# A two-layer transformer trunk on one core: inverse sums in the outputs' bank, norms by head, a two-queue launch and 512-column memory products

## The chip, the cores and the metric

The kernel runs on one core of a Trainium2 chip. The core has TensorE (PE, matrix products; its weight loads are listed as PEld), VectorE (DVE), ScalarE (ACT), GpSimd (POOL) and SyncE (SP, which issues DMAs here). Products accumulate in PSUM, eight banks of 512 fp32 columns for each of 128 partitions. The metric is the device time of one execution in microseconds, the median of several runs; lower is better.

## The reference

All is float32: 512 tokens of 1024 features, a memory of 256 tokens, two layers.

```python
for layer in range(DEPTH):                      # 2
    x = x + 0.5 * _swiglu(_rmsnorm(x, ffn_pre_norm[layer]), ffn_pre_w_gu[layer], ffn_pre_w_down[layer])
    h = _rmsnorm(x, mix_norm[layer])
    if layer % 2 == 0:
        x = x + _even_mixer(h, ...)             # stick-breaking attention and a gated unit
    else:
        x = x + _mla_mixer(h, positions, ...)   # 16 heads, low-rank q and kv
    x = x + _memory_cross_attention(_rmsnorm(x, xmem_norm[layer]), _rmsnorm(mem, xmem_mem_norm[layer]), ...)
    x = x + 0.5 * _swiglu(_rmsnorm(x, ffn_post_norm[layer]), ...)
```

The two places inside that matter here:

```python
# _mla_mixer: q and k are normed head by head (96 wide), then causal softmax attention
q = _rmsnorm(q, q_g)
k = _rmsnorm(k, k_g)
p = jax.nn.softmax(jnp.where(causal, sc, -jnp.inf), axis=-1)
# _memory_cross_attention: 4 heads of 256
k, v = jnp.split((hm @ wkv).reshape(b, m, MEM_HEADS, 2 * MEM_HEAD_DIM), 2, axis=-1)
k = _rmsnorm(k, k_g)
```

## The kernel before

x lies transposed in SBUF: eight tiles x0 to x7 of 128 features by 512 tokens. Every product is done with both operands split into a rounded high part and a low rest: `mm3` (L101) issues three products, high x high (L103), high x low (L104) and low x high (L105). `prep` (L122) makes hh and hl of x times the norm's gain; the norm's factor per token is applied later. `squares` (L136) sums x squared over the tiles into sqs; `stats` (L147) turns sqs into the factor per token (a product of 1 column by ones, then `rsqrt`, L107, a chain of some eleven small DVE operations), and `spread` (L164) copies it over all partitions into rbc.

Weights come in granules of at most 512 KB. `gran` (L85) loads one (three raw buffers), ACT casts the high part wh, and POOL (in two halves) or DVE subtracts for the low part wl (four buffers each).

The kernel's text is not the order of execution: a scheduler orders each engine's instructions by the order of the text and by when it expects their inputs. `with self.queued()` ties the PE instructions of a block behind the last mm3 issued so far. At run time each engine runs its list in order.

The stages, with their time in the profile: ffn, the even mixer, memory attention of layer 0 (its products from 592.90 us), two ffn, the MLA mixer, memory attention of layer 1 (from 1752 us), ffn.

- Launch: `constants` (L60) issues on SP the gains gc, the first weight granule (its low part made by DVE) and x0 to x7. `run` (L1112) does eight preps and eight squares. In `ffn` (L211) each product pair (gate pg, up pu) takes two PSUM banks of a pool of five; two more banks belong to psA, used by the down products, and one to the statistics. In the first ffn `stats` follows product 1 and `spread` product 2 (s0, L218).
- MLA attention (`mla_attn`, L654). Fill work, `filler`, projects q and kv for four groups of four heads (eight steps a group), then `first_half` begins the output product. `proj_q` and `proj_kv` square their result on ACT into a tile dg (one buffer), and DVE reduces it (L693, L719). When a group is complete, `norms` makes the factors, `knorm` (L670) scales all four heads of k at once, on DVE for group 0 and on POOL for the others, and POOL scales q (L700). The loop over n (L908) does, for head n: `scores` of n; for head n - 1 `weights`, which transposes the exponentials (L845) into banks of the tag pt (two banks) and copies them to wT; then `ahead`, which turns q and k of head n + 2 by transposes (L740), also into pt. In an even round two heads are complete: `inverse` transposes the inverse sums ar into a pt bank (L864), `spread` multiplies them out into the same bank (L872) and ACT copies it to rbc; `values` multiplies with v into the one bank of the tag av (L887), scales by rbc into a buffer of the tag sq, and splits. `take` puts fill steps between: FILL[n] has three counts, after the first weights, before `spread`, and at the round's end.
- Memory products (`memkv`, L959). Eight products in the order K0, K1, V0, K2, V1, K3, V2, V3; each has 256 columns, two token blocks in one bank, and two granules of four k-tiles. After the first: the memory's own statistics (L996) and `stats` of x (L1001). K products get tk (ACT), its squares, `rsqrt`, a scaling on DVE; `fin` transposes tk (L1026) two products later. V products get tv and a split. PSUM: three banks mm, three at, two psA.

Of the kernel before, what the change touches and what calls it, by code (L numbers as in the profile page):

```python
# [26 lines left out]
class Trunk:  # L27
# [32 lines left out]
    def constants(self):  # L60
        nc, cp, a = self.nc, self.cp, self.a
        self.gc = self.t(cp, [P, 10, KT], "gc")
        nc.sync.dma_start(out=self.gc, in_=a["gcols"])

        self.first = self.gran(a["w_gu0"][0], KT, P, lo="dve") if self.stop in (None, 1) else None
        self.x = [self.t(self.xp, [P, S], f"x{f}") for f in range(KT)]
        for f in range(KT):
# [3 lines left out]
        self.ones = self.t(cp, [P, P], "ones")  # L71
        nc.vector.memset(self.ones, 1.0)
        self.rbc = self.t(cp, [P, S], "rbc")

    def split(self, hi, lo, src, eng_hi="act", eng_lo="dve"):
# [7 lines left out]
        e.tensor_tensor(out=lo, in0=src, in1=hi.bitcast(F32), op=ALU.subtract)  # L83

# [126 lines left out]
    def ffn(self, w_gu, w_dn, g_next, out=None):  # L211
        nc, tc = self.nc, self.tc
        with tc.tile_pool(name=self.nm("ffn"), bufs=1) as fp, \
# [4 lines left out]
            s0 = 1 if self.first else 0  # L218
# [14 lines left out]
            for half in range(2):  # L233
                acts = []
                for j in range(H):
                    jj = half * H + j
                    pg = self.t(pp, [P, S], "mm")
                    pu = self.t(pp, [P, S], "mm")
                    for ps, w in ((pg, w_gu[jj]), (pu, w_gu[NFF + jj])):
                        wh, wl = self.first or self.gran(w, KT, P)  # L240
# [413 lines left out]
    def mla_attn(self, p, pl, pp, cT, krr, skr, gqk, neg, tq, o):  # L654
# [15 lines left out]
        def knorm(st, y, eng):  # L670
            st["ks"] = ks = self.t(p, [P, NT, G, 96], "ks", bufs=2)
            by = lambda d: y[:, :, :, None].to_broadcast([P, NT, G, d])
            eng.tensor_tensor(out=ks[:, :, :, 0:64], in0=st["kn"], in1=by(64), op=ALU.mult)
            eng.tensor_tensor(out=ks[:, :, :, 64:96], in0=krr[:, :, None, :].to_broadcast([P, NT, G, 32]), in1=by(32),
                              op=ALU.mult)

        def proj_kv(st, g, t):
# [22 lines left out]
            nc.gpsimd.tensor_tensor(out=st["qs"], in0=st["qs"], in1=st["s"][:, :, :, None].to_broadcast([P, NT, G, 96]),  # L700
                                    op=ALU.mult)

        def proj_q(st, g, t):
# [13 lines left out]
            s1 = self.t(self.sp, [P, NT, P], "dg", bufs=1)[:, :, 0:96]  # L717
# [137 lines left out]
        def inverse(sm):  # L855
# [7 lines left out]
            ps = self.t(pp, [P, S], "pt", bufs=2)  # L863
# [15 lines left out]
        def values(n, wTs, rb):  # L879
# [13 lines left out]
            w = self.t(self.sp, [P, S], "sq", bufs=2)  # L893
# [14 lines left out]
        for n in range(17):  # L908
# [50 lines left out]
    def memkv(self, p, pp, l, kT, V, gqk):  # L959
# [22 lines left out]
        for n, c in enumerate((0, 2, 1, 4, 3, 6, 5, 7)):  # L982
            h = c // 2
            ps = self.t(pp, [P, MT, 256], "mm")
            for hf in range(2):
                wh, wl = self.gran(a["xmem_wkv"][l, c * 2 + hf], 4, 256, lo="dve")
                for k in range(4):
                    kk = hf * 4 + k
                    for m in range(MT):
                        cs = slice(m * P, (m + 1) * P)  # L990
                        self.mm3(ps[:, m, :], (mh[kk][:, cs], ml[kk][:, cs]), (wh[:, k, :], wl[:, k, :]),
                                 kk == 0 and m == 0, kk == KT - 1)
            if rm is None:
                st = self.t(pp, [P, S], "at")
# [6 lines left out]
                self.stats(pp, "at")  # L1001
            while fins and fins[0][0] <= n - 2:
                with self.queued():
                    fins.pop(0)[1]()
            if c % 2 == 1:
                tv = self.t(p, [P, MT, 256], "tv", bufs=2)
                for m in range(MT):
                    nc.scalar.activation(out=tv[:, m, :], in_=ps[:, m, :], func=AF.Copy, scale=rm[:, m:m + 1])
                self.split(*V[h], tv, "dve", "pool")
                continue  # L1010
            tk = self.t(p, [P, MT, 256], "tk", bufs=2)
            ss = self.t(p, [P, MT], "kss", bufs=2)
            scr = self.t(p, [P, 256], "kscr", bufs=2)
            for m in range(MT):
                nc.scalar.activation(out=tk[:, m, :], in_=ps[:, m, :], func=AF.Copy, scale=rm[:, m:m + 1])
                nc.scalar.activation(out=scr, in_=tk[:, m, :], func=AF.Square, accum_out=ss[:, m:m + 1])
            rk = self.rsqrt(ss, MT, 1.0 / 256, EPS)
            for m in range(MT):
                nc.vector.tensor_scalar(out=tk[:, m, :], in0=tk[:, m, :], scalar1=rk[:, m:m + 1], scalar2=None,
                                        op0=ALU.mult)  # L1020

            def fin(tk=tk, h=h):
                for d in range(2):
                    pt = self.t(pp, [P, S], "at")
                    for m in range(MT):
                        nc.tensor.transpose(out=pt[:, m * P:(m + 1) * P], in_=tk[:, m, d * P:(d + 1) * P],  # L1026
                                            identity=self.ident)
                    hi, lo = kT[h][d]
# [177 lines left out]
```

## Time and profile before

| What | us |
|---|---|
| median of 3 runs | 2297.13 |
| the runs | 2290.03, 2297.13, 2308.14 |
| profiled execution | 2289.97 |
| its span | 2288.3 |
| mean granted TensorE clock in it | 0.997 |
| ACT busy in MLA attention, 1552 to 1735 (183) | 104.77 |
| DVE busy in MLA attention | 110.42 |
| DVE busy in the memory products of layer 0 (48.10) | 36.03 |
| ACT busy there | 28.49 |

A row of a list of waits reads: engine, tile and line that waited, what released it, us in total, times, longest. A row of a timeline reads: start, duration, engine, line, operation, output <- inputs, shapes, count, and in brackets the idle time before with its releaser. A PE duration holds the pipeline's depth; how far apart two products start says what one costs. A granted clock of 1.00 is full speed of TensorE. A row with several counts (x4) covers instructions one after another.

### The profile page before, as it was taken

Reading aid. Unit: us, or ns where it says so; the run is one execution under the profiler, and the core shown is the slowest. Engines: PE = TensorE matmul, PEld = TensorE weight load, DVE = VectorE, ACT = ScalarE, POOL = GpSimd, SP = SyncE. Lnnn points to the kernel's source line nnn. Section 1 sums busy time; section 2 is a strip of 40 time slices with the busy share of each in tenths; the row PEclk is TensorE's granted clock in tenths of the full one; section 3 lists DMA queues with packets and bytes.
Section 4 is the critical chain, followed back from the end, with each engine's and each line's share of the span. In section 5 each row is a group of like instructions: output and inputs, shape, how many; then the busy total and the mean of one; then the engine's idle time right before and its main releaser. Section 6 shows DMA issues by size and latency. Waiting matters only on the chain. (4 is left out here: it accounts for less than half of the span.)

```text
span 2288.3 us, 29129 instructions
## 1 busy us (share of the span) xinstructions
PE 2250.2 (98%) x11240; PEld 1885.1 (82%) x11240; DVE 907.2 (40%) x1686; ACT 867.4 (38%) x1443; POOL 1018.3 (45%) x824
## 2 busy tenths in 40 slices
PE   8999999999999999999999999998889999999999
PEld 6888888977988888888888888897668988888887
DVE  5211323466745422123422022376558555221220
ACT  4222333366544332223322232356546544322221
POOL 5545546212243454554554554635322424545543
PEclk9999999999999999999999999999999999999999
DMA  4323324211421332332332332321003412323222
GB/s 157 96 83 111 98 80 128 88 56 57 144 97 63 92 99 82 114 94 82 111 95 83 110 100 79 105 83 51 28 29 111 134 61 83 101 77 117 93 82 93
DMA packets 67354, 208.68 MB, mean 91 GB/s; under 512 B 8592, under 2 KB 10640, under 8 KB 67216
## 3 DMA queue, kind: packets, MB, share of 16 engines
q1 hardware_dynamic: 67216, 206.83, 29.3%
q8 instruction: 88, 1.44, 0.3%
q14 instruction: 50, 0.41, 0.1%
HBM read 204.70 MB, written 2.10 MB: 90 GB/s over the span
## 5 line engine op out<-in xcount | busy, mean ns | idle before, releaser
L97 POOL TENSOR_TENSOR wl<-wr,wh 128x512 fp32r<-128x512 f32 (+2 forms) x752 | 945.9, 1279 | 1083.2 <-ACT wh L92 1083.1
L92 ACT CAST wh<-wr 128x1024 fp32r<-128x1024 f32 (+3 forms) x423 | 408.0, 965 | 1040.2 <-PE mm L104 578.8
L103 PE MATMUL mm<-hh,wh 128*128 128x512 f32 x1424 | 556.6, 391 | 6.8 <-ACT hh L130 6.8
L104 PE MATMUL mm<-hl,wh 128*128 128x512 f32 x1424 | 555.6, 390 | 0.5 <-DVE hl L131 0.5
L105 PE MATMUL mm<-hh,wl 128*128 128x512 f32 x1424 | 555.5, 390 | 0.0
L103 PEld LDWEIGHTS mm<-hh,wh 128*128 128x128 f32 x1424 | 268.2, 188 | 62.3 <-ACT hh L130 6.8
L104 PEld LDWEIGHTS mm<-hl,wh 128*128 128x128 f32 x1424 | 268.2, 188 | 56.8 <-DVE hl L131 1.0
L105 PEld LDWEIGHTS mm<-hh,wl 128*128 128x128 f32 x1424 | 268.2, 188 | 56.2 <-POOL wl L97 0.3
L103 PE MATMUL A<-ah,wh 128*128 128x512 f32 x704 | 277.4, 394 | 0.0
L105 PE MATMUL A<-ah,wl 128*128 128x512 f32 x704 | 276.0, 392 | 0.0
L104 PE MATMUL A<-al,wh 128*128 128x512 f32 x704 | 273.2, 388 | 0.0
L226 DVE TENSOR_TENSOR t<-mm,rbc 128x512 f32<-128x512 f32 x88 | 60.9, 692 | 394.9 <-PE mm L105 394.9
L259 DVE SCALAR_TENSOR_TENSOR x<-A,x 128x512 f32<-128x512 f32 x64 | 44.3, 692 | 358.0 <-PE A L105 358.0
L105 PEld LDWEIGHTS A<-ah,wl 128*128 128x128 f32 x704 | 132.1, 188 | 31.0
L104 PEld LDWEIGHTS A<-al,wh 128*128 128x128 f32 x704 | 132.2, 188 | 29.6
L103 PEld LDWEIGHTS A<-ah,wh 128*128 128x128 f32 x704 | 132.3, 188 | 26.3
L224 DVE TENSOR_TENSOR t<-mm,rbc 128x512 f32<-128x512 f32 x88 | 60.9, 692 | 195.4 <-PE mm L105 188.5
L83 DVE TENSOR_TENSOR al<-t,ah 128x512 fp32r<-128x512 f32 x88 | 82.9, 942 | 60.4 <-ACT ah L79 60.4
L103 PE MATMUL A<-hh,wh 128*128 128x512 f32 x240 | 96.7, 403 | 0.0
L105 PE MATMUL A<-hh,wl 128*128 128x512 f32 x240 | 94.0, 392 | 0.0
L104 PE MATMUL A<-hl,wh 128*128 128x512 f32 x240 | 93.8, 391 | 0.0
L103 PE MATMUL mm<-wh,hh 128*128 128x256 f32 (+1 forms) x288 | 82.2, 285 | 0.0
(331 smaller groups left out, 3224.2 us busy)
## 6 DMA issues: line engine op xcount, KB each, us to landing
wr<-in_w_gu SPq DMA_DIRECT2D x176, 512.0 KB, 3.6
wr<-in_w_dn SPq DMA_DIRECT2D x64, 384.0 KB, 3.1
wr<-in_w_dn SPq DMA_DIRECT2D x64, 320.0 KB, 2.9
wr<-in_xmem_wkv SPq DMA_DIRECT2D x32, 512.0 KB, 3.3
wr<-in_xmem_wq SPq DMA_DIRECT2D x16, 512.0 KB, 3.3
wr<-in_xmem_wo SPq DMA_DIRECT2D x16, 512.0 KB, 3.2
wr<-in_sbg_w_zv SPq DMA_DIRECT2D x12, 512.0 KB, 3.6
wr<-in_sbg_w_qk SPq DMA_DIRECT2D x8, 512.0 KB, 3.6
```

The lines of the kernel that those rows point to most:

```text
L83: e.tensor_tensor(out=lo, in0=src, in1=hi.bitcast(F32), op=ALU.subtract)
L92: nc.scalar.copy(out=hi, in_=raw)
L97: e.tensor_tensor(out=lo_[:, c], in0=raw[:, c], in1=hi[:, c].bitcast(F32), op=ALU.subtract)
L103: mm(out, lhsT=A[0], rhs=B[0], start=start, stop=False, skip_group_check=True)
L104: mm(out, lhsT=A[0], rhs=B[1], start=False, stop=False, skip_group_check=True)
L105: self.pe = mm(out, lhsT=A[1], rhs=B[0], start=False, stop=stop, skip_group_check=True)
L224: nc.vector.tensor_tensor(out=t1, in0=pg, in1=self.rbc, op=ALU.mult)
L226: nc.vector.tensor_tensor(out=t2, in0=pu, in1=self.rbc, op=ALU.mult)
L259: nc.vector.scalar_tensor_tensor(out=self.x[m], in0=ps, scalar=0.5, in1=self.x[m], op0=ALU.mult, op1=ALU.add)
```

## The change

Four places change; the computation is the same.

- Launch: the ones are made first; gc and x0 are issued by ACT's queue, the first granule by SP in two parts (the first two k-tiles, then six), each split as its x tile is prepared; x1 to x7 follow on SP. Twelve products of the ones with themselves are issued to PE. The first product pair takes psA's banks, and `stats` and `spread` of the first ffn move to after products 3 and 4.
- MLA: the squares of q and kv go to tiles of the tag sq (two buffers) instead of dg, and `values` scales into dg. `knorm` works head by head, and POOL's scaling of q goes with it. `inverse` uses the av bank. In even rounds the fill steps of the round's end stand between `spread` and `values`.
- Memory: four products of 512 columns (K of heads 0 and 1, K of 2 and 3, V of 0 and 1, V of 2 and 3), each in two banks, one per token block, with four granules of two k-tiles; `fin` of one head after the third and one after the fourth granule of the next product; `stats` of x after the second product. PSUM: four banks mm, two at.
- The memory weights' layout in HBM follows.

```diff
     def constants(self):
...
-        nc.sync.dma_start(out=self.gc, in_=a["gcols"])
-        self.first = self.gran(a["w_gu0"][0], KT, P, lo="dve") if self.stop in (None, 1) else None
+        nc.vector.memset(self.ones, 1.0)
...
+        nc.scalar.dma_start(out=self.gc, in_=a["gcols"])
+        nc.scalar.dma_start(out=self.x[0], in_=a["xT"][0])
+        self.first = self.first_gran(a["w_gu0"][0]) if self.stop in (None, 1) else None
+        for f in range(1, KT):
             nc.sync.dma_start(out=self.x[f], in_=a["xT"][f])
+        ps = self.psA()
+        for _ in range(12):
+            nc.tensor.matmul(ps[:, 0:P], lhsT=self.ones, rhs=self.ones, start=True, stop=True)
         self.ident = self.t(cp, [P, P], "ident")
         make_identity(nc, self.ident)
...
+    def first_gran(self, src):
+        nc = self.nc
+        raw = self.t(self.wr, [P, KT * P], "wr")
+        hi = self.t(self.ws, [P, KT * P], "wh", F32R)
+        lo = self.t(self.ws, [P, KT * P], "wl", F32R)
+        parts = (slice(0, 2 * P), slice(2 * P, KT * P))
+        for c in parts:
+            nc.sync.dma_start(out=raw[:, c], in_=src[:, c])
+        def split(i):
+            self.split(hi[:, parts[i]], lo[:, parts[i]], raw[:, parts[i]])
+        r = lambda z: z.rearrange("p (k c) -> p k c", k=KT)
+        return r(hi), r(lo), split
...
-            s0 = 1 if self.first else 0
+            s0 = 3 if self.first else 0
...
-                    pg = self.t(pp, [P, S], "mm")
-                    pu = self.t(pp, [P, S], "mm")
+                    pg, pu = [self.psA() if self.first else self.t(pp, [P, S], "mm") for _ in range(2)]
...
         def knorm(st, y, eng):
...
+            for h in range(G):
+                by = lambda d: y[:, :, h, None].to_broadcast([P, NT, d])
+                eng.tensor_tensor(out=ks[:, :, h, 0:64], in0=st["kn"][:, :, h], in1=by(64), op=ALU.mult)
+                eng.tensor_tensor(out=ks[:, :, h, 64:96], in0=krr, in1=by(32), op=ALU.mult)
+                nc.gpsimd.tensor_tensor(out=st["qs"][:, :, h], in0=st["qs"][:, :, h],
+                                        in1=st["s"][:, :, h, None].to_broadcast([P, NT, 96]), op=ALU.mult)
...
-            s2 = self.t(self.sp, [P, NT, P], "dg", bufs=1)[:, :, 0:64]
+            s2 = self.t(self.sp, [P, S], "sq", bufs=2).rearrange("p (g d) -> p g d", g=G)[:, :, 0:64]
...
-            s1 = self.t(self.sp, [P, NT, P], "dg", bufs=1)[:, :, 0:96]
+            s1 = self.t(self.sp, [P, S], "sq", bufs=2).rearrange("p (g d) -> p g d", g=G)[:, :, 0:96]
...
         def inverse(sm):
...
-            ps = self.t(pp, [P, S], "pt", bufs=2)
+            ps = self.t(pp, [P, S], "av", bufs=1)
...
         def values(n, wTs, rb):
...
-            w = self.t(self.sp, [P, S], "sq", bufs=2)
+            w = self.t(self.sp, [P, NT, P], "dg", bufs=1).rearrange("p t c -> p (t c)")
...
-            take(FILL[n][1])
             if len(wTs) == 2:
                 with self.queued():
                     rb = spread()
+                take(FILL[n][1] + FILL[n][2])
                 with self.queued():
                     values(n - 2, wTs, rb)
                 wTs = []
-            take(FILL[n][2])
+            else:
+                take(FILL[n][1] + FILL[n][2])
...
     def memkv(self, p, pp, l, kT, V, gqk):
...
+        for c in range(4):
+            ps = [self.t(pp, [P, 2, 256], "mm", bufs=4) for _ in range(MT)]
+            for q in range(4):
+                wh, wl = self.gran(a["xmem_wkv"][l, c * 4 + q], 2, 512, lo="dve")
+                for k in range(2):
+                    kk = q * 2 + k
                     for m in range(MT):
                         cs = slice(m * P, (m + 1) * P)
+                        self.mm3(ps[m].rearrange("p h n -> p (h n)"), (mh[kk][:, cs], ml[kk][:, cs]),
+                                 (wh[:, k, :], wl[:, k, :]), kk == 0, kk == KT - 1)
+                if q > 1 and fins:
+                    with self.queued():
+                        fins.pop(0)()
             if rm is None:
...
-                self.stats(pp, "at")
...
+            if c == 1:
+                with self.queued():
+                    self.stats(pp, "at", 2)
+            if c > 1:
+                for i in range(2):
+                    tv = self.t(p, [P, MT, 256], "tv", bufs=2)
+                    for m in range(MT):
+                        nc.scalar.activation(out=tv[:, m, :], in_=ps[m][:, i, :], func=AF.Copy, scale=rm[:, m:m + 1])
+                    self.split(*V[2 * c - 4 + i], tv, "dve", "pool")
+                continue
+            for i in range(2):
+                tk = self.t(p, [P, MT, 256], "tk", bufs=4)
...
+                fins.append(fin)
...
         for f in range(KT):
+            if self.first and f < 2:
+                self.first[2](f)
             self.prep(first, f)
```

More of the change, by code (lines that the diff above doesn't have):

```diff
@@ L236, in ffn @@
                     jj = half * H + j
-                    pg = self.t(pp, [P, S], "mm")
-                    pu = self.t(pp, [P, S], "mm")
+                    pg, pu = [self.psA() if self.first else self.t(pp, [P, S], "mm") for _ in range(2)]
                     for ps, w in ((pg, w_gu[jj]), (pu, w_gu[NFF + jj])):
-                        wh, wl = self.first or self.gran(w, KT, P)
+                        wh, wl = self.first[:2] if self.first else self.gran(w, KT, P)
                         self.first = None
@@ L1011, in memkv @@
[L1011 to L1028, printed above, removed]
-                    col = gqk[:, d:d + 1]
-                    nc.scalar.activation(out=hi, in_=pt[:, 0:M], func=AF.Copy, scale=col)
-                    nc.vector.scalar_tensor_tensor(out=lo, in0=pt[:, 0:M], scalar=col, in1=hi.bitcast(F32),
-                                                   op0=ALU.mult, op1=ALU.subtract)
@@ L1034, in memkv, with fin @@
-            fins.append((n, fin))
+                    self.stats(pp, "at", 2)
[8 more added lines that the diff above has]
+                tk = self.t(p, [P, MT, 256], "tk", bufs=4)
+                ss = self.t(p, [P, MT], "kss", bufs=2)
+                scr = self.t(p, [P, 256], "kscr", bufs=2)
+                for m in range(MT):
+                    nc.scalar.activation(out=tk[:, m, :], in_=ps[m][:, i, :], func=AF.Copy, scale=rm[:, m:m + 1])
+                    nc.scalar.activation(out=scr, in_=tk[:, m, :], func=AF.Square, accum_out=ss[:, m:m + 1])
+                rk = self.rsqrt(ss, MT, 1.0 / 256, EPS)
+                for m in range(MT):
+                    nc.vector.tensor_scalar(out=tk[:, m, :], in0=tk[:, m, :], scalar1=rk[:, m:m + 1], scalar2=None,
+                                            op0=ALU.mult)
+                def fin(tk=tk, h=2 * c + i):
+                    for d in range(2):
+                        pt = self.t(pp, [P, S], "at", bufs=2)
+                        for m in range(MT):
+                            nc.tensor.transpose(out=pt[:, m * P:(m + 1) * P], in_=tk[:, m, d * P:(d + 1) * P],
+                                                identity=self.ident)
+                        hi, lo = kT[h][d]
+                        col = gqk[:, d:d + 1]
+                        nc.scalar.activation(out=hi, in_=pt[:, 0:M], func=AF.Copy, scale=col)
+                        nc.vector.scalar_tensor_tensor(out=lo, in0=pt[:, 0:M], scalar=col, in1=hi.bitcast(F32),
+                                                       op0=ALU.mult, op1=ALU.subtract)
+                fins.append(fin)
@@ L1184, in _layouts @@
     o["inv_freq"] = A(np.broadcast_to((10000.0 ** (-np.arange(16) / 16.0)).astype(np.float32), (P, 16)))
-    for n, nk, nc in (("xmem_wq", KT, P), ("xmem_wkv", 4, 256), ("xmem_wo", 4, 256)):
+    for n, nk, nc in (("xmem_wq", KT, P), ("xmem_wo", 4, 256)):
         o[n] = A(np.stack([grans(i[n][l], nk, nc) for l in range(2)]))
+    kv = i["xmem_wkv"].reshape(2, D, 4, 2, 256).transpose(0, 1, 3, 2, 4).reshape(2, D, 2048)
+    o["xmem_wkv"] = A(np.stack([grans(kv[l], 2, 512) for l in range(2)]))
     o["xg"] = A(np.stack([np.concatenate([cols(i["xmem_q_gain"][l]), cols(i["xmem_k_gain"][l])], axis=1)
```

28 lines of the change are left out of this document (2 added, 26 removed).

## The prediction

> **What bounds the kernel now.** I read the page first, for the engine that the time belongs to.
>
> ```profile
> span 2288.3 us, 29129 instructions
> PE 2250.2 (98%) x11240; PEld 1885.1 (82%) x11240; DVE 907.2 (40%) x1686; ACT 867.4 (38%) x1443; POOL 1018.3 (45%) x824
> ```
>
> TensorE (PE) is busy 98% of the span; no other engine reaches half. The change removes few products, so it can win only where PE waits or runs slowly. Next I read who PE waits for, and then stretches of time with the granted clock.
>
> ```profile
> PE pt L740 <- DVE qTl L83: 9.7, 7, 1.4
> PE mm L103 <- ACT hh L130: 6.8, 1, 6.8
> PE pt L740 <- DVE wT L852: 3.6, 8, 0.9
> PE A L103 <- ACT dg L718: 3.0, 1, 3.0
> ...
> PE st L152 <- DVE sqs L145: 2.0, 1, 2.0
> PE at L152 <- DVE sqs L145: 1.4, 1, 1.4
> ```
>
> ```profile
> 25.40:28.70 3.30, 3.30 (x10) 2.53 (x9) 3.23 (x3) 0.07 (x1) 3.30 (x3) 0.50 0.70 232
> ...
> 1650.10:1653.40 3.30, 3.30 (x16) 1.24 (x12) 0.38 (x1) 0.08 (x1) 0.00 (x0) 0.50 0.00 0
> 1674.00:1677.30 3.30, 3.30 (x15) 1.33 (x11) 0.31 (x1) 0.06 (x1) 0.00 (x0) 0.50 0.00 0
> 1694.50:1697.80 3.30, 3.30 (x12) 1.15 (x13) 0.75 (x1) 0.88 (x2) 0.00 (x0) 0.50 0.00 0
> ```
>
> The waits (total, times, longest) are some 26 us, in the launch, the MLA stage and one memory stage. A stretch's row gives its length, the busy time of PE, PEld, DVE, ACT and POOL, and then the granted clock: four stretches of at least 3.3 us ran at 0.50. Waits and half of those stretches make 33 us, 1.4% of the span: apart from the narrower gain of the memory products, this is the whole pool that the change draws on.
>
> **1. The launch.** The next rows are the start: engine, line, tile, and in brackets the idle time before and its releaser.
>
> ```profile
> 5.06 1.04 ACT L92 CAST wh<-wr 128x1024 fp32r<-128x1024 f32 x1 [2.98 <-DMA wr<-in_w_gu]
> 8.25 3.41 ACT L130 ACTIVATE hh<-x,gc 128x512 fp32r<-128x512 f32 x5 [0.29 <-DMA x<-in_xT]
> 11.23 0.60 PE L105 MATMUL mm<-hh,wl 128*128 128x512 f32 x1
> 12.09 1.14 ACT L144 ACTIVATE sq<-x 128x512 f32<-128x512 f32 x2
> 13.13 1.03 ACT L92 CAST wh<-wr 128x1024 fp32r<-128x1024 f32 x1
> 14.24 14.72 POOL L97 TENSOR_TENSOR wl<-wr,wh 128x512 fp32r<-128x512 f32 x10 [12.87 <-ACT wh L92]
> 15.59 0.19 PEld L105 LDWEIGHTS mm<-hh,wl 128*128 128x128 f32 x1 [0.26 <-POOL wl L97]
> 20.49 0.39 PE L105 MATMUL mm<-hh,wl 128*128 128x512 f32 x1
> 22.93 1.05 PE L152 MATMUL st<-ones,sqs 128*128 128x1 f32 x8 [2.05 <-DVE sqs L145]
> ```
>
> And two rows of an undisturbed run of 512-column products, four steps apart: (642.93 - 642.02) / 4 = 0.2275 us a step.
>
> ```profile
> 642.02 0.39 PE L105 MATMUL A<-hh,wl 128*128 128x512 f32 x1
> ...
> 642.93 0.39 PE L103 MATMUL A<-hh,wh 128*128 128x512 f32 x1
> ```
>
> The split first weight, x[0] and the gains on the ACT queue and the 12 warm-up products let PE begin sooner than the 6.8 us of the wait row. ACT's two added DMA issues fall into its 2.98 us of idling; SP issues one DMA more and two fewer ahead of x[1]; POOL, which now makes the identity later, idles 12.87 us before its first wl. I give this little. The first product needs all eight x tiles, and ACT was already waiting for their DMA (0.29). Behind it the second product needs its own wh and wl: ACT finished hh at 11.66 (8.25 + 3.41), did the first squares, cast wh at 13.13, and POOL's first half gave PE its wl at 15.59, 3.93 us after the last hh. That chain stays. PE ended its first product near 15.1 (15.59 less two steps), having run slowly until 11.23 (0.60 for a product against 0.39); fed as fast as x arrives it would end soon after the last hh, near 12.4, 2.7 earlier, and then wait for wl. If the split brings the last hh forward by 0.5 us, the start gains 0.5. Bounds: 2.7 if ACT casts the second wh before the squares; a loss of 1.6 if the new idle time brings another slow stretch (priced below).
>
> The statistics of x move from after the second product to after the fourth (s0 from 1 to 3). Their wait is 22.93 - 20.49 = 2.44, less one step: 2.2 us. By the fourth product, two products of 24 steps or 10.9 us later, the sums on DVE are long done. The first pair of products sits in the two psA banks, so no bank is short. The 0.50 stretch that follows costs half of its 3.3 us, 1.6, and goes with the wait. Launch: 0.5 + 2.2 + 1.6 = **4.3 us**.
>
> [...]
>
> **2. MLA attention.** One even round, then two odd ones, then the same values products in a slow stretch.
>
> ```profile
> 1600.27 0.38 PE L845 MATMUL pt<-ident,pb 128*128 128x128 f32 x2
> 1600.72 0.28 PE L864 MATMUL pt<-ident,ar 128*16 128x128 f32 x1
> ...
> 1603.21 0.64 PE L740 MATMUL pt<-ident,ks 128*96 128x128 f32 x4 [1.40 <-DVE qTl L83]
> 1603.78 0.66 PE L872 MATMUL pt<-arT,asel 16*128 16x128 f32 x4
> 1604.37 2.37 PE L887 MATMUL av<-wT,vs 128*64 128x512 f32 x16
> ```
>
> ```profile
> 1592.75 0.38 PE L845 MATMUL pt<-ident,pb 128*128 128x128 f32 x2
> ...
> 1594.28 0.48 PE L103 MATMUL A<-wh,ch 128*128 128x512 f32 x1
> ```
>
> ```profile
> 1614.26 0.44 PE L845 MATMUL pt<-ident,pb 128*128 128x128 f32 x2 [0.69 <-DVE wT L852]
> ...
> 1616.85 0.42 PE L103 MATMUL A<-wh,ch 128*128 128x384 f32 x1
> ```
>
> ```profile
> 1649.49 4.00 PE L887 MATMUL av<-wT,vs 128*64 128x512 f32 x16
> ```
>
> In an even round the inverse (ar) holds one of the two pt banks until spread, so ks gets the bank of qs only when DVE has read it: the 1.40. From the last weights transposes to spread it takes 1603.78 - 1600.27 = 3.51 us. An odd round has the same three users of pt without ar: 1.53 us in the good case, 2.59 in the bad one. With ar in the av bank an even round becomes an odd one plus a transpose step of 0.11 (0.38 for two, 0.28 for one, rounded up) and some 0.2 before spread: 1.84 or 2.90. It saves 1.67 or 0.61, in the six even rounds that turn two heads ahead (2 to 12). Five good and one bad: 5 x 1.67 + 0.61 = 9.0; round 14 has only the wait behind ar and saves perhaps 0.5. Bounds: 6 x 0.61 = 3.7 and 6 x 1.67 + 0.5 = 10.5.
>
> New wait: values can now start only when ACT has copied spread out of av (before, it had its own bank). The fill moved between them, 6 products of 0.23 (1.4 us) or more, covers the copy unless ACT is late; I charge 1.0 for eight rounds, bounds 0 and 8 x 0.6.
>
> The slow stretches: 4.00 against 2.37 for the same 16 products, 1.6; three of them, each behind an even round's wait, about 4.5 in all. I take them as gone, bounds 0 and 4.9.
>
> The 3.0 us wait for dg: ACT's Square had one buffer, and DVE's reduction of it stood behind the norms of group 0.
>
> ```profile
> 1548.18 3.24 DVE L674 TENSOR_TENSOR ks<-krr,rs_y 128x512 f32<-128x512 f32 x1
> ...
> 1588.38 2.00 POOL L97 TENSOR_TENSOR wl<-wr,wh 128x384 fp32r<-128x384 f32 x2 [10.65 <-ACT wh L92]
> ```
>
> Two sq buffers let it run one tile ahead, and norms by head are shorter, so reductions can come between: 2.5, bounds 0 and 3.0. Norms by head issue 12 operations for 3 per group; PE waits for none of them today, and POOL then idles 10.65 us (last row), so they cost and gain nothing directly. If that cover went, a few us of POOL time would stand ahead of the first turn of a group. MLA: 9.0 + 0.5 + 4.5 + 2.5 - 1.0 = **15.5 us**.
>
> [...]
>
> **3. The memory products.**
>
> ```profile
> 592.90 0.28 PE L103 MATMUL mm<-wh,mh 128*128 128x256 f32 x1
> ...
> 598.60 0.50 PE L996 MATMUL at<-ones,msqs 128*128 128x1 f32 x4
> ...
> 641.12 0.60 PE L1026 MATMUL at<-ident,tk 128*128 128x128 f32 x4
> ```
>
> ```profile
> 607.95 0.61 DVE L1019 TENSOR_SCALAR tk<-tk,rs_y 128x256 f32<-128x256 f32 x2
> ```
>
> A layer's 384 products of 256 columns, with 24 small ones of some 0.11, take 641.12 - 592.90 = 48.22 us: (48.22 - 2.6) / 384 = 0.1188 each. Each of the 192 new ones takes a step of 0.2275 and saves 2 x 0.1188 - 0.2275 = 0.010: 1.9 a layer, 3.8 for both. DMAs and casts stay as many. x's sums come after the second product, when DVE has them: the 1.4 us wait goes.
>
> Against that: the transposes of head 0 now come three granules (3 x 12 x 0.2275 = 8.2 us) after its product, where two products of 598.60 - 592.90 = 5.7 us lay between. Today its tk was ready 608.56 - 598.60 = 9.96 us after, with x's sums in between on DVE. So up to 1.8 us a layer may be lost, less if DVE is freer; I charge 0.75 a layer. Bounds 0 and 3.6 for both. Memory: 3.8 + 1.4 - 1.5 = **3.7 us**.
>
> **Sum.** 4.3 + 15.5 + 3.7 = 23.5. The profiled execution took 2289.97 (span 2288.3), so 2266.5 in its terms. The three runs have a median of 2297.13, from 2290.03 to 2308.14; the four executions together have their middle at 2293.6. I take the sum from there: 2270.
>
> **The rivals.**
> - *The wait on pt stays in another form* (ks behind the weights' bank, or values behind the copy of spread on ACT). For it: the bad odd round. Against it: the good ones. At the low bounds, 3.7 instead of 9.5 and 3.0 more for the copy: 8.8 less, 2279. Chance 0.18.
> - [...] Chance 0.12.
> - *The launch starts early throughout* (second wh before the squares, 2.2 more), no wait in the memory products (1.5 more), copy always covered (1.0), all rounds good (1.5): 6 more, 2264. Chance 0.07.
> - *Slower: post-processing of two heads stands ahead of the next granule on ACT and DVE*, so that PE waits at each of the eight memory products. For it: one K product brings DVE four wl subtractions, two chains of rsqrt and four scalings at once. Against it: four split buffers hold three granules, 8.2 us, ahead. A wait as long as the 9.96 us chain, 8 x (9.96 - 2.7) = 58 less 23.5, gives 2328; it decides from 3 us a product (8 x 3 = 24). Chance 0.03.
>
> **How the numbers follow.** The forecast has 0.60 and its own range of 2262 to 2277. One per cent, about what a measurement of this kernel can tell from no change, is 23 us: below 2274 counts as faster. Of the forecast some 0.52 lies there; with the early launch and a little of the slow-stretch rival, faster is 0.62. Same is 0.35, slower 0.03. The bounds of the unknown terms and the scatter of the runs widen the range to 2256 to 2286.
>
> **What would show it.** Right: no wait of qTl above 0.9 in even rounds, ar writing av; spread then six or more products, then values; no wait of 2 us before the statistics and no 0.50 stretch near 25 us; no wait of 3 us for a Square's buffer; memory layers near 46 us. Wrong: PE idle before values for rbc, L1026's transposes waiting for tk, 0.50 stretches as before, or the second product of the launch beginning well before 15 us.

## The result, and the profile after

| What | before | after |
|---|---|---|
| median of 5 runs, us | 2297.13 | 2278.43 |
| the runs | 2290.03 to 2308.14 | 2277.22 to 2279.39 |
| profiled execution, and its span | 2289.97, 2288.3 | 2278.58, 2276.9 |

The ratio is 0.9913, 95% interval 0.9891 to 0.9935: 18.7 us off the median, 0.9%. Profile against profile it is only 11.4 us; why the two differ is shown by the second profile of before, below. The time lies 8.4 us above the forecast of 2270. It is inside the stated range of 2256 to 2286, and 1.4 us outside the forecast's own range of 2262 to 2277.

From here on, lines are those of the kernel after: mm3 is L123 to L125, the turn L761, the weights L866 and L873, ar L885, spread L893, the copy rbc L896, values L908, norms by head L695 to L697, the squares of q L739 with their reduction L740, the memory's key transposes L1053. In runs whose edit adds or removes lines these numbers are shifted by a few. First the head of the page after, and the list of what PE waited for (total, times, longest):

```profile
span 2276.9 us, 28456 instructions
PE 2249.0 (99%) x10880; PEld 1868.0 (82%) x10880; DVE 899.4 (40%) x1693; ACT 867.3 (38%) x1444; POOL 1016.8 (45%) x854
```

```profile
PE at L1053 <- DVE tk L1046: 5.2, 3, 2.2
PE A L123 <- ACT sq L739: 4.2, 1, 4.2
PE pt L761 <- DVE wT L873: 3.9, 6, 1.1
...
PE pt L761 <- DVE qTl L88: 0.6, 1, 0.6
```

The waits of before for x at the start (6.8), for the sums of x (2.0 and 1.4) and of the turn for qTl (9.7 us in seven waits) are gone or small. Two new ones lead: the transposes of tk, which the prediction had at 1.5, and the one wait for a Square's buffer, which it had at 0.5 and which has grown from 3.0 to 4.2.

The stretches after (length, busy PE, PEld, DVE, ACT, POOL, granted clock, DMA share and GB/s): the two at 0.50, each with the 3.4 us ahead of it.

```profile
1547.80:1551.20 3.40, 1.38 (x6) 0.76 (x5) 3.40 (x4) 0.48 (x1) 3.40 (x4) 1.00 0.00 0
1551.20:1558.10 6.90, 4.63 (x14) 3.43 (x14) 3.75 (x8) 3.79 (x10) 6.74 (x9) 0.51 0.17 57
1776.50:1779.90 3.40, 1.53 (x7) 0.91 (x5) 3.33 (x6) 1.27 (x2) 2.69 (x2) 1.00 0.30 118
1779.90:1783.40 3.50, 3.16 (x10) 2.70 (x11) 2.47 (x5) 1.59 (x3) 0.00 (x0) 0.51 0.26 62
```

The four of before are gone. Of the two that are there now, one (6.83 us by the clock's record) stands behind the wait for sq and one (3.41) in the second memory stage, behind a wait for tk.

Where the time went, by first instructions on PE in the two profiles:

| Stretch | before | after | difference | predicted |
|---|---|---|---|---|
| start to the even mixer's first z product | 464.21 | 459.97 | -4.24 | -4.3 |
| from there to the first memory product | 128.69 | 128.68 | 0 | 0 |
| layer 0's memory products to the first transpose of cq (MLA) | 929.40 | 931.97 | +2.57 | -1.1 |
| MLA to layer 1's first memory product | 230.01 | 217.50 | -12.51 | -15.5 |
| layer 1's memory products to the last product | 531.70 | 534.46 | +2.76 | -2.6 |

The launch came out as forecast, MLA 3 us short, and the memory products lost 5.3 us where 3.7 were to be gained.

An even round after (compare it with the round at 1600 of before):

```profile
1580.89 0.38 PE L866 MATMUL pt<-ident,pb 128*128 128x128 f32 x2
1581.11 0.27 PE L885 MATMUL av<-ident,ar 128*16 128x128 f32 x1
1581.21 0.60 PE L761 MATMUL pt<-ident,qs 128*96 128x128 f32 x4
1581.79 0.64 PE L761 MATMUL pt<-ident,ks 128*96 128x128 f32 x4
1582.36 0.66 PE L893 MATMUL av<-arT,asel 16*128 16x128 f32 x4
...
1585.25 2.38 PE L908 MATMUL av<-wT,vs 128*64 128x512 f32 x16
```

No row has an idle time in brackets: qs and ks each find a bank. ("..." stands for fill products.) Last weights to spread takes 1582.36 - 1580.89 = 1.47 us, against 3.51. The six even rounds that turn took 3.57, 3.51, 3.56, 3.50, 3.80 and 3.51 before, and 1.47, 1.51, 1.47, 1.51, 1.47 and 1.47 after: 12.5 us less. Values start 0.26 to 0.33 us behind the fill, without waiting for rbc.

The place of the 4.2 us: VectorE's list in group 0, then ACT's square that waits for it, then PE.

```profile
1545.36 0.42 DVE L695 TENSOR_TENSOR ks<-kn,rs_y 128x256 f32<-128x256 f32 x1
1545.70 0.93 DVE L696 TENSOR_TENSOR ks<-krr,rs_y 128x128 f32<-128x128 f32 x1
1546.55 1.05 DVE L695 TENSOR_TENSOR ks<-kn,rs_y 128x256 f32<-128x256 f32 x1
...
1552.22 1.65 DVE L740 TENSOR_REDUCE ssqk<-sq 128x4 f32<-128x384 f32 x3
...
1545.59 3.55 POOL L697 TENSOR_TENSOR qs<-qs,sqr 128x384 f32<-128x384 f32 x4 [2.55 <-DVE sqr L721]
1549.10 2.17 POOL L117 TENSOR_TENSOR wl<-wr,wh 128x384 fp32r<-128x384 f32 x2
...
1552.79 0.49 ACT L739 ACTIVATE sq<-A 128x384 f32<-128x384 f32 x1 [4.50 <-DVE ssqk L740]
1553.34 0.79 PE L123 MATMUL A<-wh,ch 128*128 128x512 f32 x1 [4.16 <-ACT sq L739]
```

The first norm, begun before POOL's, takes 0.42; the same operation 1 us later, with POOL at work, 1.05. Eight such operations fill 1545.36 to 1552.3, and the reduction that frees the buffer stands behind all eight: the reductions did not come between. The two whole operations of before took 4.46 together, and a reduction came right behind them:

```profile
1547.04 1.22 DVE L673 TENSOR_TENSOR ks<-kn,rs_y 128x1024 f32<-128x1024 f32 x1
1548.18 3.24 DVE L674 TENSOR_TENSOR ks<-krr,rs_y 128x512 f32<-128x512 f32 x1
```

The memory products: steps in an undisturbed run, and the wait for tk of the last key head.

```profile
596.55 0.39 PE L124 MATMUL mm<-wl,mh 128*128 128x512 f32 x1
...
599.57 0.40 PE L125 MATMUL mm<-wh,ml 128*128 128x512 f32 x1
...
626.90 2.69 POOL L88 TENSOR_TENSOR vl<-tv,vh 128x512 fp32r<-128x512 f32 x2 [46.19 <-DVE rs_u L137]
...
627.14 1.25 DVE L138 SCALAR_TENSOR_TENSOR rs_u<-rs_u,rs_v 128x2 f32<-128x2 f32 x1
628.42 1.19 DVE L139 SCALAR_TENSOR_TENSOR rs_y<-rs_u,rs_y 128x2 f32<-128x2 f32 x1
...
630.14 0.63 PE L1053 MATMUL at<-ident,tk 128*128 128x128 f32 x4 [2.24 <-DVE tk L1046]
```

A step is (599.57 - 596.55) / 13 = 0.232, not 0.2275. And two operations on two columns, 0.16 us elsewhere on this list, take 1.25 and 1.19 while POOL makes vl: 2.1 us more, about as long as PE stands (2.24). The same pair of rows stands at 1777.25 in layer 1, ahead of a wait of 2.21. The third wait for tk, 0.76 at 1759.93, is of the first key head, with no work on POOL beside it.

### The profile page after: what moved, and what is told of

The parts are those of the page before. It is cut to its first block, busy times and chain, and to the rows that moved or that the text cites. A ratio compares the mean times of both kernels' runs of the same rounds, so it can differ in the third digit from the quotient of the medians.

```text
span 2276.9 us, 28456 instructions
## 1 busy us (share of the span) xinstructions
PE 2249.0 (99%) x10880; PEld 1868.0 (82%) x10880; DVE 899.4 (40%) x1693; ACT 867.3 (38%) x1444; POOL 1016.8 (45%) x854
## 5 line engine op out<-in xcount | busy, mean ns | idle before, releaser
L112 ACT CAST wh<-wr 128x1024 fp32r<-128x1024 f32 (+2 forms) x422 | 406.9, 965 | 1053.1 <-PE mm L124 579.3
L123 PE MATMUL mm<-hh,wh 128*128 128x512 f32 x1408 | 548.7, 390 | 0.0
L125 PE MATMUL mm<-hh,wl 128*128 128x512 f32 x1408 | 547.9, 389 | 0.0
L124 PE MATMUL mm<-hl,wh 128*128 128x512 f32 x1408 | 547.8, 389 | 0.0
L125 PEld LDWEIGHTS mm<-hh,wl 128*128 128x128 f32 x1408 | 264.3, 188 | 54.8
L123 PEld LDWEIGHTS mm<-hh,wh 128*128 128x128 f32 x1408 | 264.4, 188 | 54.6
L123 PE MATMUL A<-ah,wh 128*128 128x512 f32 x704 | 277.4, 394 | 0.0
L125 PE MATMUL A<-ah,wl 128*128 128x512 f32 x704 | 276.0, 392 | 0.0
L125 PEld LDWEIGHTS A<-ah,wl 128*128 128x128 f32 x704 | 132.1, 188 | 31.0
L123 PEld LDWEIGHTS A<-ah,wh 128*128 128x128 f32 x704 | 132.3, 188 | 26.3
L123 PE MATMUL A<-hh,wh 128*128 128x512 f32 x256 | 103.2, 403 | 0.7 <-ACT hh L150 0.5
L124 PE MATMUL A<-hl,wh 128*128 128x512 f32 x256 | 100.3, 392 | 0.8 <-DVE hl L151 0.8
L125 PE MATMUL A<-hh,wl 128*128 128x512 f32 x256 | 100.4, 392 | 0.6 <-POOL wl L117 0.6
L123 PE MATMUL mm<-wh,hh 128*128 128x256 f32 (+1 forms) x288 | 82.2, 285 | 0.0
```

Source lines behind the costliest of these rows:

```text
L112: nc.scalar.copy(out=hi, in_=raw)
L123: mm(out, lhsT=A[0], rhs=B[0], start=start, stop=False, skip_group_check=True)
L124: mm(out, lhsT=A[0], rhs=B[1], start=False, stop=False, skip_group_check=True)
L125: self.pe = mm(out, lhsT=A[1], rhs=B[0], start=False, stop=stop, skip_group_check=True)
```

## The experiments

The base is the kernel after, unless another is named; differences in us are from its median of 2278.43, and the ratios are to the kernel before, measured beside each on the same chip. The kernel after was not run again beside them, and before's medians there lie between 2294.96 and 2298.33. So a difference of 2 to 4 us rests on the waits in the profiles more than on the times: the runs with GpSimd's key norms and with group 0 normed whole overlap those of after, and only with the inverse sums in pt and with the old order of the fill does a ratio's interval lie apart from after's.

**The memory products as before** (memkv and its weight layout put back whole):

```diff
...
-        for c in range(4):
...
+        for n, c in enumerate((0, 2, 1, 4, 3, 6, 5, 7)):
...
```

> The changed kernel with the memory products, their order and their weights' layout of the kernel before; all else stays changed. Theory A (the memory part is a loss: transposes wait for tk, 5.2 us in all, and a slow stretch follows in layer 1): about 4 us faster than the changed kernel's 2278.4, near 2274; layer 0 from its first product to the first query projection takes 48.6 instead of 51.0 us, the waits for tk are gone, x's 1.4 us wait of layer 1 is back. Rival B (the memory part gained as forecast and the loss sits elsewhere): 2 to 4 us slower, near 2281.

2275.25 (ratio to before 0.9907, interval 0.9887 to 0.9927), 3.2 less than after. From the first memory product to the first query projection the first layer takes 48.57, as in the kernel before, against 51.02 with the change. So the new memory products are a loss as they stand.

**The key transposes one granule later:**

```diff
-                if q > 1 and fins:
+                if fins and c * 4 + q >= fins[0][0]:
...
-                fins.append(fin)
+                fins.append((c * 4 + 7 + i, fin))
```

> The changed kernel with each head's transposes one granule (2.8 us) later in the text: head 0 after the fourth granule of the next product, head 1 after the first of the one after, and so for heads 2 and 3. Theory A1 (the transposes stood too early on PE's list for the chain of rsqrt on DVE): the waits for tk fall from 5.2 us to under 1, the 0.50 stretch of layer 1 goes, 4 to 6 us faster than 2278.4. Rival A2 (DVE has too much to do, and what waits changes only its name): the same sum of waits in the memory products, under tk or under wl, and the time within 1.5 us of 2278.4.

2272.52 (0.9898, 0.9878 to 0.9917): 5.9 less. No wait for tk is left, and layer 0's products take 48.40. So the place of the transposes was the loss, not the width of the product. A new entry shows what comes next: x's own sums wait until VectorE has read a bank of "at".

```profile
PE at L172 <- DVE kl L1058: 2.0, 2, 1.7
```

**Group 0's key norms on GpSimd:**

```diff
-            knorm(st, y[:, 0], nc.vector if g == 0 else nc.gpsimd)
+            knorm(st, y[:, 0], nc.gpsimd)
```

> The changed kernel with the norms of group 0 on POOL, as those of the other groups, head by head. Theory C1 (DVE's eight norm operations of group 0 take about 1 us each because POOL works at the same time, 6.9 us in all, and DVE's reduction that frees the squares' buffer stands behind them): the 4.2 us wait of the projection for the square's buffer goes to under 1, the slow stretch behind it goes too, 4 to 6 us faster than 2278.4. Rival C2 (the two sq buffers are too few whatever DVE does): the wait stays above 3 us. Rival C3: the first turn of group 0 then waits for POOL, which has some 7.5 us of norms, and the wait only moves to the turn.

2276.16 (0.9915, 0.9890 to 0.9940): 2.3 less. The wait for sq is gone, but a part of it has moved, as rival C3 had it, to the turn. It now waits for POOL; the profile names a weight's low part, which stands right behind the norms there:

```profile
PE pt L761 <- POOL wl L117: 2.8, 1, 2.8
```

**Group 0 normed whole, the other groups by head:**

```diff
+            if eng is nc.vector:
+                by = lambda d: y[:, :, :, None].to_broadcast([P, NT, G, d])
+                eng.tensor_tensor(out=ks[:, :, :, 0:64], in0=st["kn"], in1=by(64), op=ALU.mult)
...
+                return
```

> The changed kernel with group 0 normed whole, two operations on DVE and one on POOL as before, the other groups head by head. Theory C1: the two DVE operations end some 2 us earlier than the eight, so the 4.2 us wait falls to about 2; 1.5 to 3 us faster than 2278.4. Rival C2: the wait stays at 4.2, the time too. Should it rise, the norms by head had shortened it.

2275.26 (0.9911, 0.9891 to 0.9932): 3.2 less. The wait for sq falls from 4.2 to 1.6, and in this profile no stretch at 0.50 is left in MLA.

**One half whole, the other by head.** Which by-head operations cost, VectorE's or GpSimd's? First only GpSimd's scale of q is made whole in group 0:

> In group 0 the key norms stay by head on VectorE (eight small operations), and the scale of the queries on GpSimd is one whole operation again instead of four. Theory (VectorE stands behind GpSimd once for each small operation, whatever the size of GpSimd's): the eight operations still take 5 to 7 us, the reduction behind them is late as before, and TensorE's wait for sq stays at 3 to 4.5 us; time as the kernel after, within 2 us. Rival (GpSimd's four operations are the cost): the eight take some 4 us and the wait falls to 2 us or less, 3 us faster.

2281.15 (0.9923, 0.9894 to 0.9951), 2.7 more than after; the wait for sq is 5.8, above what either theory expected. VectorE's second operation, begun 0.10 after GpSimd's one long one, took 2.85 and ended 0.15 after it:

```profile
1545.85 0.42 DVE L695 TENSOR_TENSOR ks<-kn,rs_y 128x256 f32<-128x256 f32 x1
1546.18 2.85 DVE L696 TENSOR_TENSOR ks<-krr,rs_y 128x128 f32<-128x128 f32 x1
1548.95 1.23 DVE L695 TENSOR_TENSOR ks<-kn,rs_y 128x256 f32<-128x256 f32 x1
...
1546.08 2.80 POOL L701 TENSOR_TENSOR qs<-qs,sqr 128x1536 f32<-128x1536 f32 x1 [2.55 <-DVE sqr L725]
1548.84 2.18 POOL L117 TENSOR_TENSOR wl<-wr,wh 128x384 fp32r<-128x384 f32 x2
```

Then only the key norms are whole:

> The other half: in group 0 the key norms are two whole operations on VectorE, the scale of the queries stays by head on GpSimd. Theory: two operations stand behind GpSimd at most twice; together they take 2.5 to 4.5 us (4.47 with both whole), the reduction runs by 1550, TensorE's wait for sq falls to 1.6 us or less as with both whole, and the half-clock stretch behind it may go: 2 to 4 us faster than the kernel after. Rival: the wait stays above 3 us, so that by-head operations on GpSimd are what delays.

2274.74 (0.9894, 0.9870 to 0.9917), 3.7 less. The two norms take 2.5 us together, and PE does not wait for sq at all:

```profile
1547.03 1.22 DVE L695 TENSOR_TENSOR ks<-kn,rs_y 128x1024 f32<-128x1024 f32 x1
1548.16 1.32 DVE L696 TENSOR_TENSOR ks<-krr,rs_y 128x512 f32<-128x512 f32 x1
1549.41 1.65 DVE L746 TENSOR_REDUCE ssqk<-sq 128x4 f32<-128x384 f32 x3
```

The wait for sq puts the four cases in order. Few large operations on VectorE and small ones on GpSimd is the best of them: 0.0, against 1.6 with both whole, 4.2 with both by head, and 5.8 the other way round. In time the first two can't be told apart (2274.74 and 2275.26).

**The inverse sums back in a pt bank:**

```diff
-            ps = self.t(pp, [P, S], "av", bufs=1)
+            ps = self.t(pp, [P, S], "pt", bufs=2)
```

> The kernel after with the transpose of the inverse sums back in a bank of pt (the spread with it); everything else as after, the fill between spread and values included. Theory: the bank of pt that the inverse sums held was what the next turn waited for: in the six even rounds with a turn the time from the last weights' transposes to the spread returns from 1.47-1.51 to about 3.5 us (+12 us), waits of the turn for qTl above 0.9 us return, and so may one to three stretches of 3.4 us at half clock (+1.7 each): 2290 to 2296 us in all. Rival: the new place of the values and the one-bank turn already remove the conflict; then the rounds stay near 1.5 us and the time within 2 us of the kernel after.

2300.85 (1.0021, 1.0002 to 1.0040): 22.4 more, above the expected range. The six rounds take 3.57 us again, 12.5 more in all, and the turn's waits are back:

```profile
1581.95 0.38 PE L866 MATMUL pt<-ident,pb 128*128 128x128 f32 x2
...
1584.94 0.64 PE L761 MATMUL pt<-ident,ks 128*96 128x128 f32 x4 [1.39 <-DVE qTl L88]
1585.52 0.71 PE L893 MATMUL pt<-arT,asel 16*128 16x128 f32 x4
```

```profile
PE pt L761 <- DVE qTl L88: 9.2, 7, 1.4
PE pt L761 <- DVE wT L873: 6.3, 12, 1.1
```

Most of the rest are stretches at 0.50: six in this profile, 20.5 us long (10.2 lost), where after has 10.2 (5.1 lost). That makes 17.6 of the 19.8 us between the two profiles. The runs spread again, from 2291.93 to 2304.49.

**The old order of the fill** (one part of the fill ahead of spread, values right behind spread, the other part behind them):

```diff
+            take(FILL[n][1])
             if len(wTs) == 2:
                 with self.queued():
                     rb = spread()
-                take(FILL[n][1] + FILL[n][2])
                 with self.queued():
                     values(n - 2, wTs, rb)
                 wTs = []
-            else:
-                take(FILL[n][1] + FILL[n][2])
+            take(FILL[n][2])
```

> The kernel after, with the values right behind the spread and the filling product behind the values, as in the kernel before; the inverse sums stay in av. Theory: the values then wait in each of eight even rounds for ACT's copy of the spread sums (0.58 us) with its semaphores, 0.8 to 1.0 us each: +6 to +8 us, 2284 to 2287 us. Rival: PE's values are bound elsewhere (the wT casts, v), and the copy hides: no more than 2 us.

2289.68 (0.9964, 0.9945 to 0.9983): 11.3 more, above the 2284 to 2287 that were expected. In seven of eight rounds values start 0.94 to 0.99 behind spread's last product, where before they went on after 0.2 to 0.27, with the wait that was expected,

```profile
PE av L908 <- ACT rbc L896: 4.9, 7, 0.7
```

some 5 us. The MLA stage, from the first transpose of cq to layer 1's first memory product, takes 223.60 against 217.50: 6.1 more, as expected. The other 5.4 lie in the two memory stages, whose text is unchanged: the wait for tk is 7.6 here instead of 5.2, and the profile has six stretches at 0.50 (20.5 us) where after has two (10.2). Why tk comes later there stays open. So the new order is worth some 6 us in MLA, and the inverse's place in av pays without it too: 223.60 is still 6.4 less than the 230.01 of before.

**The launch without the 12 warm-up products**, profiled twice (the second a single run):

```diff
-        ps = self.psA()
-        for _ in range(12):
-            nc.tensor.matmul(ps[:, 0:P], lhsT=self.ones, rhs=self.ones, start=True, stop=True)
```

> The kernel after without the 12 warm-up products on ones. Theory of the prediction: the start is set by the second product's chain on ACT and POOL (squares, cast of wh, subtraction for wl), so that the warm-up is worth next to nothing: the second product's first wl weight load stays near 15.3 us and the time within 1 us of the kernel after. Rival: the warm-up is what opens TensorE's clock; without it the first product runs at 0.60 us instead of 0.39 for most of its 24 steps and ends later than wl arrives: first wl load of the second product 1 to 2.5 us later and the whole kernel 1 to 2.5 us slower. [...]

> The kernel without the warm-up products once more, for a second profile: in the first its x landed so late that ACT's first hh began at 7.12 instead of 5.59. Theory (the late x was chance, the warm-up is worth nothing): with the first hh near 5.6 the first product runs at half clock to about 12, yet ends before the second product's wl arrives near 15.3; the second product's first wl load is within 0.4 us of the kernel after, relative to the first hh 9.7 us. Rival: relative to the first hh it comes 10.5 us or later, since PE is still in the first product.

2279.92 (0.9928, 0.9904 to 0.9952), 1.5 more, and 2278.84. The first hh (x times its gain, on ACT) and the first product that needs the second wl, in the second of these profiles and then in after:

```profile
6.01 0.72 ACT L147 ACTIVATE hh<-x,gc 128x512 fp32r<-128x512 f32 x1 [2.50 <-DMA x<-in_xT]
...
15.69 0.50 PE L122 MATMUL A<-hh,wl 128*128 128x512 f32 x1
```

```profile
5.59 0.72 ACT L150 ACTIVATE hh<-x,gc 128x512 fp32r<-128x512 f32 x1 [1.56 <-DMA x<-in_xT]
...
15.26 0.50 PE L125 MATMUL A<-hh,wl 128*128 128x512 f32 x1 [0.63 <-POOL wl L117]
```

From first hh to that product it is 9.68 and 9.67 us (9.69 in the other profile without warm-up, whose x landed 1.5 us later). Without the warm-up PE ran the first products at 0.63 and 0.79 us (first profile) instead of 0.40 to 0.50, and still was in time for wl. Full clock is granted from 5.01 us in after, and from 12.72 and 12.21 without the warm-up. It is worth nothing here, since ACT's and POOL's chain sets the second product. In the ten profiles with the warm-up the first hh begins between 5.53 and 6.18, so the 6.01 without it is nothing unusual. Only the 7.12 of the first profile lies outside, and whether that is chance stays open.

**The kernel before, profiled again:**

> The kernel before, unchanged, for a second profile, since its runs spread over 18 us and those of the kernel after over 2. Theory: its waits are the same from run to run, and what differs is how many stretches at half clock (3.4 us, 1.7 us lost each) follow them: a run that is 8 us longer than the first profile's 2290 shows about five more such stretches, with the waits for qTl and wT at the same 9.7 and 3.6 us within 1. Rival: the waits themselves or the DMA differ by microseconds at the same number of stretches.

2298.12, span 2296.4, 8.1 more than its first profile. The waits agree (qTl 9.7 in both, wT 4.0 against 3.6, dg 3.0 in both). The stretches at 0.50 don't agree: they last 30.7 us by the clock's record against 13.7. Half of the difference is lost, 8.5 us. Rows of three of them, with the 3.4 us ahead of the first:

```profile
1550.30:1553.70 3.40, 0.40 (x3) 0.31 (x3) 2.84 (x3) 0.90 (x2) 1.46 (x1) 1.00 0.00 0
...
1553.70:1557.20 3.50, 3.50 (x10) 2.73 (x9) 0.96 (x3) 2.95 (x7) 3.11 (x4) 0.51 0.05 9
...
1697.10:1703.90 6.80, 6.80 (x25) 3.56 (x26) 1.01 (x2) 1.27 (x2) 0.00 (x0) 0.50 0.00 0
1765.30:1772.20 6.90, 6.90 (x34) 6.90 (x34) 4.38 (x26) 0.63 (x2) 0.00 (x0) 0.51 0.58 207
```

So the 18 us between the runs of before are these stretches, and the first profile was one of its luckier executions. Over 34 executions of before, the span goes with the share of clock lost (1 - mean granted clock, times the span) with a slope of 0.97 and a correlation of 0.95.

**The mended kernel:** later key transposes, group 0 normed whole, and x's own sums at the tenth granule:

```diff
...
+                if c == 2 and q == 1:
+                    with self.queued():
+                        self.stats(pp, "at", 2)
...
-            if c == 1:
...
-                with self.queued():
-                    self.stats(pp, "at", 2)
...
```

> Two mendings together and one more: the memory's key transposes one granule later (by itself -5.9 us), group 0's norms whole instead of by head (by itself -3.2 us), and x's own sums moved from behind the second column group to the tenth granule, where no key transposes stand before them (the 2.0 us wait for kl, shown in the run with later transposes, should go). Theory: the three gains are of separate stages and add: 2278.4 - 5.9 - 3.2 - 1.5 = about 2268 (2266 to 2270). Rival: the stalls merge or move, as the wait for the squares did when the norms went to GpSimd; then 2271 to 2274, with a new wait of 2 us or more in the list of waits, or a new stretch at half clock.

2267.29, from 2266.46 to 2268.56 (0.9878, 0.9844 to 0.9911): 11.1 less than after, and the fastest of all. The parts add: 2267.8 was their sum. The wait for tk is gone from the top of its list of waits, and that for sq is small,

```profile
PE pt L769 <- DVE wT L881: 4.0, 6, 1.2
PE A L123 <- ACT sq L747: 1.6, 1, 1.6
...
PE pt L769 <- DVE qTl L88: 1.3, 1, 1.3
```

and outside the launch and the last 3 us of this profile no stretch at 0.50 is left. From the first memory product to the first query projection the layers take 47.71 and 48.95, against 48.57 and 50.16 before. The better half, key norms whole and q's scale by head, was not tried together with the other two.

## Why the prediction was right or wrong

- **The launch (4.3): right**, 4.24. The chain to the second product stayed, and the wait for the sums of x went with the stretch at 0.50 behind it. The product's wl reached PE at 15.26, 0.33 earlier, where 0.5 was given; this is less than the 0.65 by which the first hh varies between profiles, so no run shows that term. The sum has no term for the warm-up, and the warm-up bought nothing: its 12 products, 24 records, take 4.78 us, and full clock is granted from 5.01 us instead of 12.72 and 12.21, but from the first hh to the second product's wl it is 9.67 us with it and 9.68 and 9.69 without.
- **The six even rounds (9.0): right in mechanism, too small in size**, 12.5. The step that failed is the round's new length, 1.84 in the good case and 2.90 in one bad one; it is 1.47 to 1.51 in all six. The gain is above the stated bound of 10.5 as well. No bad round came: in none of the six does the turn wait long for a bank. That ar's bank was the cause is shown by the run with ar back in pt (3.57). Round 14 saved nothing where 0.5 was put.
- **Values waiting for rbc (1.0 lost): 0**; the filling product covers the copy, and without that order values wait some 5 us and MLA takes 6.1 longer. (The prediction's first rival gives 3.0 for its low bound; 8 x 0.6 - 1.0 is 3.8.)
- **The stretches at 0.50 (4.5 gained): the three went.** The chance of 0.12 was for stretches that stay, 4.5 us less. No run shows this term: the string of transposes of an even round is still there, 1.47 us long, and no stretch follows it in after. Part of the gain may be where the waits fall, which is the author's estimate: in two of the runs above, with the same rounds, a stretch of 3.41 stands at 1612.53 (memory products as before) and at 1610.62 (key norms whole), amid the waits of an odd round (0.92 and 1.12). And another of 6.83 us came behind the wait for sq, which gives back 3.4.
- **The wait for dg (2.5 gained): wrong in sign.** The failed step is "norms by head are shorter, so reductions can come between", with "they cost and gain nothing directly". They did not come between, and eight operations took 6.9 us where two took 4.5: the first took 0.42, and the seven others, with GpSimd at work, 0.82 to 1.21 each. The wait grew by 1.2. The other half of the step, the second buffer, did help: with the norms whole again the wait is 1.6, against 3.0 with the one buffer of before. With the new stretch MLA comes to 12.5 + 5.1 (three stretches, half of 10.2) - 3.4 - 1.2 = 13.0, against 12.5 measured.
- **The memory products (3.7 gained): wrong in sign**, 5.3 lost. Two steps failed. The product's step is 0.232, not the 0.2275 taken from another stage: 192 x (2 x 0.1188 - 0.232) = 1.1 a layer instead of 1.9. And the transposes waited 5.2 us for tk, above the bound of 3.6, since that bound was worked out for the first key head alone (9.96 against 8.2 us). The two long waits are of the last head: its tk is ready 18.3 us after the last step of its product (630.26 - 611.98, and the same in layer 1). On VectorE two chains of `rsqrt` and that of x's sums stand interleaved, with the weights' subtractions between, and at the end two operations stretch beside GpSimd's vl. That this stretching decides the wait is argued from its size (2.1 against 2.24), not tested by itself. In layer 1 a stretch at 0.50 followed (1.7). The wait for x's own sums did go (1.4). These terms make 3.3 of the 5.3 us. Another 1.2 is in nine steps of layer 0, which take 0.31 to 0.53 each instead of 0.232; the rest is not assigned. Transposes waiting for tk were on the prediction's own list of signs that it is wrong.
- **The time as a whole.** 23.5 was forecast in the profile's own terms and 11.4 came, less than half: 9.0 of the difference is the memory's, 3.0 MLA's. That the median still lies in the range owes much to luck. The median gained 18.7, because before's profile lay 7.2 under its median and after loses little to chance; and the rounds' gain of 3.5 over the forecast covers part of the memory's loss. The time is near the 2279 of the first rival, but by other causes: that rival's wait on pt did not come. Chances: "faster by over 1%" had most of them (0.62); 0.9913 lies within 1%, which had 0.35, though its interval reaches just past it (0.9891).

## What to carry to other kernels

Splitting an operation on VectorE into small ones so that others can come between did not pay here: the order did not let them between, and a small operation beside GpSimd cost about what GpSimd's own took, mostly some 1 us and once 2.85. Look at the order and at GpSimd's list before splitting. Where a result is moved to fewer and larger batches, count how late the input of the last consumer comes, not of the first, with those longer durations, and put the consumer one batch later: not doing so cost 5.9 us here. And a wait's price is not its length: look for the half-clock stretch behind it (here 1.7 us lost in each 3.413 at 0.50).

## What the runs showed of the hardware

**VectorE beside GpSimd.** Operations of 0.16 and 0.42 us took 1.2 and 1.05 while GpSimd worked, and one took 2.85 beside a GpSimd operation of 2.80. That one ended at 1549.03 (the run with q's scale whole), just behind the GpSimd operation that had begun before it and ended at 1548.88. In after, each of the seven norms at 1545.70 to 1551.48 also ended 0.15 to 0.29 us behind a GpSimd operation that had begun before it. VectorE's reductions took 0.55 each beside GpSimd (1.65 for three at 1552.22), as they do without it (0.54 at 1544.14). What ties the two engines was not shown.

**The stretches at 0.50 begin whole steps apart.** By the clock's records those of before begin at 25.338, 1650.082, 1673.975 and 1694.455 and last 3.413 each: 476, 7 and 6 steps of (1694.455 - 25.338) / 489 = 3.4133 us. In after they begin at 1551.248 and 1779.941, 67 steps apart, and last 6.827 and 3.413. In before again they begin, from 24.57, 448, 467, 471, 481, 490 and 510 steps later. Counted in these steps from the span's start, the remainders are 1.44, 1.59 and 0.68 us: they differ from run to run.

A cell is one step of 3.4133 us, laid from the beginning of a stretch. Past the launch, in before and after, the two cells at full clock with PE busy for 1.34 and 1.50 us were followed by a cell at 0.50 (the rows at 1547.80 and 1776.50, whose ends are rounded, have 1.38 and 1.53). Of the eight with 1.67 to 2.11, the three with 1.79, 2.02 and 2.02 were, and those with 1.67, 1.76, 2.05, 2.08 and 2.11 were not. No cell above that was. In before again the cells ahead of the six stretches past the launch have 0.40 to 2.10. In the mended kernel the cell at 1543.70 had PE busy for 1.8 us, and none followed it:

```profile
1543.70:1547.10 3.40, 1.80 (x10) 1.18 (x8) 3.31 (x4) 1.23 (x4) 3.40 (x3) 1.00 0.00 0
```

What ends a stretch was not worked out: two in before's second profile last 6.83 us though PE is busy throughout (the rows at 1697.10 and 1765.30).

So the waits of before, which agree in both profiles (qTl 9.7 and 9.7, wT 3.6 and 4.0, dg 3.0 and 3.0), had 13.7 us at 0.50 behind them in one execution and 30.7 in the other, half of it lost. That this goes by where a wait falls among the cells is the author's estimate from these rows; no run tests it by itself.
